# A hybrid backbone on one core: tiles moved by a few bytes in SBUF, a new start-up order, and idle products of the identity

## The chip, the cores and the metric

The kernel runs on one core of one Trainium2 chip. The metric is device time in microseconds. In the profile PE is TensorE (matrix products), PEld its loads of the stationary operand, DVE is VectorE, ACT is ScalarE, POOL is GpSimd and SP is the queue that issues the DMAs.

## The reference, cut to what matters

Two streams of 256 tokens of width 1024 (context and latent) pass four layers. The mixers are: gated delta net (layer 0), short convolution (1), differential attention (2), gated delta net (3). A squared-ReLU MLP follows each. Everything is float32.

```python
for i in range(DEPTH):                                   # DEPTH = 4, D = 1024
    mod = silu(c) @ ada_w[i] + ada_b[i]                  # shifts, scales, gates
    h = rmsnorm(x, norm1_g[i]) * (1 + sc1) + sh1
    x = x + g1 * mixer[i % 3](h)                         # delta net, conv, attention, delta net
    h = rmsnorm(x, norm2_g[i]) * (1 + sc2) + sh2
    x = x + g2 * (square(relu(h @ w1)) @ w2)             # w1: 1024 x 4096
return rmsnorm(x, final_g)                               # latent tokens; in layer 3 the context is dropped
```

## The kernel before

Activations lie transposed: eight tiles `x0..x7` of 128 features by 512 tokens (context in columns 0 to 255, latent in 256 to 511). Float32 products are split: `h` is kept as `hh` + `hl`, a weight tile as `whi` + `wlo`, and `prod` issues three products in the float32r type: hh by whi, hl by whi, hh by wlo. In a row `ch<-u,wlo`, `u` is the moving operand that streams through the array, `wlo` the stationary one, and `ch`, `mm` and `po` are PSUM banks. A product has 512 columns when both streams are computed together and 256 when one is. Every product has its own load of the stationary operand (128 columns).

Weights come as 512 KB tiles `raw` through SP. `splitter` casts them on ACT (`whi`) and subtracts on DVE or POOL (`wlo`). The last weight tiles of a stage go to tiles of their own, `whix0..` and `wlox0..`, in the stage's pool.

`mlp` runs eight rounds `f`. Each computes four blocks of `h @ w1` (4 x 8 x 3 = 96 products), squares them into `u` (`u_fin`), and then multiplies the `u` of the round before with `w2` (8 blocks x 4 x 3 = 96 products). So 96 products on `hh`/`hl` and 96 on `u` alternate. In layers 0 to 2 both kinds have 512 columns, but for the last `w2` round, which takes `whix`/`wlox` and 256 columns; in layer 3 all have 256.

The delta net keeps its per-head outputs in `y` and `NT`, the convolution in `yh` and `yl`; products with the output weights read those.

At the start `consts` loads `cv` (the conditioning vector), `more_consts` the eight `x` tiles and `pack` (all small constants), and `ada` streams 16 tiles `adaw` of the modulation weights, each followed by eight narrow passes on PE (`ch<-adaw,s`). `first_squares` sums the squares of `x` in `nacc` for the first norm. The products of layer 0's first four weight tiles (`joint`) are interleaved with those of `adaw`. When the 16 tiles are used, `opened` is set and the delta net opens its pool; the other 32 modulation tiles (`Z<-in_ada_w`) go through its ring of `Z` slots.

The order on every engine is written by a list scheduler (`Issue.run`): strands with priorities yield operations, and the one with the earliest modelled start is emitted. So a changed cost or a new strand changes what follows. Semaphores keep each engine's order as emitted.

Of the kernel before, what the change touches and what calls it, by code (L numbers as in the profile page):

```python
# [397 lines left out]
class Net:  # L398
# [4 lines left out]
    HP, DHP = -20, -20  # L403
    SHARE = 0.7
    RAW = 3
    RINGS = (dict(u=4, kt=2, E=2, qd=1, NT=2, scr=2, Z=5, gate=2, o=3, NY=1),
             dict(u=4, kt=3, E=3, qd=3, NT=3, scr=3, Z=4, gate=4, o=4, NY=1))

    def __init__(self, tc, ctx, a, depth=4):
        self.tc, self.nc, self.ctx, self.a, self.depth = tc, tc.nc, ctx, a, depth  # L410
        self.I = Issue(tc.nc)
        pool = lambda name, bufs, **k: ctx.enter_context(tc.tile_pool(name=name, bufs=bufs, **k))
        self.cp = pool("cp", 1)
        self.wp = pool("wp", 1)
# [3 lines left out]
        self.whome, self.wheld, self.wpool = [], deque(), None  # L418
# [47 lines left out]
    def splitter(self):  # L466

        I = self.I
        for n, (ap, kc, cols) in enumerate(self.wlist):
            self.pump_raw()  # L470
            home = self.whome[n]
            if home:
                yield [self.wt[n], lambda: BIG if self.wpool is None else 0.0]
            else:
                yield [self.wt[n], lambda: BIG if sum(m > self.wdone for m in self.wheld) >= self.NW else 0.0,
                       lambda: I.slot(self.wp, "whi", self.NW) - 300.0]
                self.wheld.append(n)
# [12 lines left out]
            self.wsplit = n + 1  # L490
# [249 lines left out]
    def norm_strand(self, i, which, st, half, h):  # L740

        I = self.I
        yield from self.norm_rs(st, half)
        rs, r, c = st["rs"][half], 1 - half, HALF[half]
        if "A" not in st:
# [4 lines left out]
        for k in range(NCH):  # L750
# [13 lines left out]
            B = mod[:, 24 * which + k, r:r + 1]  # L764
            yield I.act(h[0][k][:, c], tmp, AF.Identity, bias=B)
            if late:
                yield I.stt(*late)
                I.rel(late[1])
            late = (h[1][k][:, c], tmp, B, h[0][k][:, c].bitcast(F32), ALU.add, ALU.subtract)
        yield I.stt(*late)  # L770
        I.rel(late[1])
        st["hev"][half].on = True

    def norm_start(self, i, which, st, halves=(0, 1)):
        I = self.I
        h = ([], [])
        for k in range(NCH):
            h[0].append(I.tile(self.sp, f"hh{k}", [P, TT], F32R))
            h[1].append(I.tile(self.sp, f"hl{k}", [P, TT], F32R))
        st["hev"] = [Event(), Event()]  # L780
        st["h"] = h
        for half in halves:
            I.spawn(self.norm_strand(i, which, st, half, h), 3 + half)


# [6 lines left out]
    def block(self, wn, rhs, kc, cols, ps, s=slice(0, P), m=P, off=0):  # L792


        c = slice(cols.start - off, cols.stop - off)
        yield [self.have(wn)]
# [4 lines left out]

    def joint(self, wns, rhs, parts=HALF):

# [7 lines left out]
        for c in parts:  # L811
            for k in range(NCH - self.LATE if c is parts[-1] else NCH):
                for wn, ps in group:
                    yield from self.joint_prod(wn, ps, rhs, c, k)
        return group, rhs, parts[-1]

    def joint_prod(self, wn, ps, rhs, c, k):
        yield [self.have(wn)]
        wh, wl = self.wt[wn]
        m = wh.shape[-1]  # L820
        yield [wh, wl, rhs[0][k][:, c], rhs[1][k][:, c]]
        yield from self.prod(ps[0:m, c], wh[:, k, :], wl[:, k, :], rhs[0][k][:, c], rhs[1][k][:, c], k == 0, k == NCH - 1)

    def joint_end(self, group, rhs, c, fin):

        for n, (wn, ps) in enumerate(group):
            for k in range(NCH - self.LATE, NCH):
                yield from self.joint_prod(wn, ps, rhs, c, k)
            self.done(wn)
# [55 lines left out]
    def mlp(self, i, t0, st, nst, pl):  # L885
# [3 lines left out]
        h = st["h"]  # L889
        first = yield from self.joint(pl[0, 0], h, [HALF[x] for x in halves])  # L890
        with self.tc.tile_pool(name=f"mlp{i}", bufs=1) as up:
            us = {}
            self.wpool = up
            ada = Event(i + 1 == self.depth)
# [6 lines left out]
            def u_fin(f, m, ps):  # L901
                yield [lambda: I.slot(up, "r", 2)]
                r = I.tile(up, "r", [P, TT], F32, 2, True)
                u = I.tile(up, "u", [P, TT], F32, 2, True)
                yield I.act(r[:, cols], ps[:, cols], AF.Relu)
                I.rel(ps)
                yield I.act(us[f][0][m][:, cols], r[:, cols], AF.Square)
                yield I.act(u[:, cols], r[:, cols], AF.Square)
                yield I.vtt(us[f][1][m][:, cols], u[:, cols], us[f][0][m][:, cols].bitcast(F32), ALU.subtract)
                I.rel(r, u)  # L910

            nf = FF // 512
            for f in range(nf):
# [3 lines left out]
                for m in range(0 if f else 4, 4):  # L917
                    yield [self.mm_slot()]
                    ps = self.mm_ps()
                    yield from self.block(pl[0, f][m], h, NCH, cols, ps)  # L920
                    self.done(pl[0, f][m])
                    I.spawn(u_fin(f, m, ps), 2)
                if f:
                    yield from self.proj_rounds(i, pl[1, f - 1], 4, 2, us.pop(f - 1), t0, 40, None)
            if i + 1 < self.depth:
                self.norm_start(i + 1, 0, nst)
            yield from self.proj_rounds(i, pl[1, nf - 1], 4, 2, us.pop(nf - 1), t0, 40, nst)
            self.wpool = None
# [19 lines left out]
    def sconv_mixer(self, i, j, st, nst, pl):  # L948
# [3 lines left out]
        with self.tc.tile_pool(name=f"sc{i}", bufs=1) as sc:  # L952
            self.wpool = sc
            yh = [I.tile(sc, f"yh{m}", [P, TT], F32R) for m in range(NCH)]
# [66 lines left out]
    def gdn_mixer(self, i, j, last, st, nst, pl):  # L1021
# [6 lines left out]
        with self.tc.tile_pool(name=f"gd{i}", bufs=1) as gp:  # L1028
# [15 lines left out]
            for step, s in enumerate(self.ORDER[j]):  # L1044
# [27 lines left out]
                else:  # L1072
# [3 lines left out]
                    if final:  # L1076
                        self.norm_start(i, 1, nst, (1,) if t0 else (0, 1))
                    y = [sum((list(self.y[m // 2][x]) for m in heads[::2]), []) for x in range(2)]
# [277 lines left out]
    def gated(self, n, o):  # L1356
# [8 lines left out]
        if last:  # L1365

            yield [self.made[H - 1], self.free("NT", 2)] if 3 not in self.y else []
            if 3 not in self.y:
                y = [self.take("NT", [P, 2, TT], F32R) for x in range(2)]
                self.y[3] = [[y[x][:, m, :TT - t0] for m in range(2)] for x in range(2)]  # L1370
# [228 lines left out]
    def diff_head(self, n, qk, evs):  # L1599
# [38 lines left out]
        I.rel(po)  # L1638
        if n // 4 not in self.y:
            self.y[n // 4] = tuple([I.tile(dp, f"y{x}{m}", [P, TT], F32R, self.NYD) for m in range(4)] for x in range(2))  # L1640
        yh, yl = self.y[n // 4]
# [38 lines left out]
    def trunk(self):  # L1680
# [26 lines left out]
        for k in range(NCH):  # L1707
# [4 lines left out]
            I.rel(o)  # L1712

    def first_squares(self, st, half):
        for k in range(NCH):
# [3 lines left out]
    def run(self):  # L1719
        with self.tc.manual_schedule():  # L1720
# [116 lines left out]
```

## Time and profile before

| | us |
|---|---|
| median of three timed runs (lowest, highest) | 2559.81 (2558.70, 2560.28) |
| the profiled execution's own time | 2558.65 |
| its span, first to last instruction | 2556.8 |
| PE busy in the span | 2486.0 |
| DVE, ACT, POOL busy | 1874.3, 1224.3, 381.6 |

Matmul records overlap, since products are pipelined and their ends are modelled. So the time from the start of one product to the start of the next says more than the duration of a record: a run of products that follow each other without a wait has the length of the run divided by their number as its spacing.

### The profile page before, as it was taken

How to read it: one execution, taken by the hardware profiler on the slowest of the kernel's cores; microseconds unless marked ns; L12 is line 12 of the kernel's file. 1: busy time of each engine (PE TensorE's matmuls, PEld its weight loads, DVE VectorE, ACT ScalarE, POOL GpSimd, SP SyncE). 2: the span in 40 equal slices, each digit the busy share in tenths (PEclk: the TensorE clock that was granted, in tenths of full speed). 3: DMA queues.
4: the chain of work that ended last, by engine and by line, in shares of the span. 5: the costliest groups of instructions: out<-in, count | busy, mean ns of one | idle time of the engine just before them, and what ended most of it. 6: DMA issues, size and time to landing. Idle time of an engine off the chain costs nothing.

```text
span 2556.8 us, 41944 instructions
## 1 busy us (share of the span) xinstructions
PE 2486.0 (97%) x16396; PEld 2091.7 (82%) x16396; DVE 1874.3 (73%) x3552; ACT 1224.3 (48%) x2280; POOL 381.6 (15%) x273
## 2 busy tenths in 40 slices
PE   7999999899999999999999999999999999998998
PEld 3778787888888988888889767888888978888998
DVE  5776777699955545999746666799965688786666
ACT  4675664543333333533243554543233576665554
POOL 0444534100000000000000000000000164454000
PEclk9999999899999999999999999999999999998999
DMA  7322222366634233566432322366633121122564
GB/s 295 104 67 71 93 70 84 124 222 221 209 97 124 67 93 105 198 213 216 148 93 79 95 66 70 116 203 217 209 121 125 57 68 35 51 60 83 174 184 129
DMA packets 91638, 323.30 MB, mean 126 GB/s; under 512 B 10288, under 2 KB 13872, under 8 KB 91056
## 3 DMA queue, kind: packets, MB, share of 16 engines
q1 hardware_dynamic: 91440, 320.62, 38.7%
q8 instruction: 129, 2.11, 0.3%
q14 instruction: 69, 0.57, 0.1%
HBM read 317.44 MB, written 1.05 MB: 125 GB/s over the span
## 4 chain that ended last, share of the span: by engine, by line
PE 88%; DVE 6%; ACT 3%; DMA 2%; issue 1%; POOL 0%; SPq 0%; DVEq 0%; ACTq 0%; POOLq 0%
PE ch L236 43%; PE mm L236 41%; PE po L236 2%; PE ch L244 1%; DVE Z L269 1%; DMA adaw<-in_ada_w 1%; DVE wlo L274 1%; DVE dsm L290 1%; ACT L181 1%; ACT whi L257 0%; DVE e L277 0%; DVE x L277 0%; DVE nacc L274 0%; ACT kt L253 0%; DVE e L286 0%
## 5 line engine op out<-in xcount | busy, mean ns | idle before, releaser
L257 ACT CAST whi<-raw 128x1024 fp32r<-128x1024 f32 x380 | 399.6, 1052 | 806.4 <-PE ch L236 427.7
L274 DVE TENSOR_TENSOR wlo<-raw,whi 128x1024 fp32r<-128x1024 f32 x305 | 376.1, 1234 | 228.8 <-ACT whi L257 217.7
L236 PE MATMUL mm<-hh,whi 128*128 128x512 f32 (+1 forms) x1344 | 486.0, 362 | 0.0
L236 PE MATMUL mm<-hl,whi 128*128 128x512 f32 (+1 forms) x1344 | 485.4, 361 | 0.0
L236 PE MATMUL mm<-hh,wlo 128*128 128x512 f32 (+1 forms) x1344 | 484.0, 360 | 0.9 <-DVE wlo L274 0.9
L281 DVE CUSTOM_DVE_ANT_0 adaj<-adat,adas,pack 128x1024 bf16<-128x1024 f32 x288 | 368.7, 1280 | 9.5 <-ACT adas L253 5.7
L236 PE MATMUL ch<-u,whi 128*128 128x512 f32 (+1 forms) x1024 | 287.2, 367 | 0.0
L236 PE MATMUL ch<-hh,whi 128*128 128x512 f32 (+3 forms) x784 | 281.3, 359 | 2.1 <-ACT hh L253 2.1
L236 PEld LDWEIGHTS mm<-hh,wlo 128*128 128x128 f32 x1344 | 256.5, 191 | 32.6 <-issue 4.9
L236 PEld LDWEIGHTS mm<-hh,whi 128*128 128x128 f32 x1344 | 256.7, 191 | 30.5 <-issue 3.1
L236 PE MATMUL ch<-hh,wlo 128*128 128x512 f32 (+3 forms) x784 | 281.2, 359 | 0.0
L236 PEld LDWEIGHTS mm<-hl,whi 128*128 128x128 f32 x1344 | 256.7, 191 | 29.8 <-issue 3.0
L236 PE MATMUL ch<-hl,whi 128*128 128x512 f32 (+3 forms) x784 | 280.8, 358 | 0.2 <-DVE hl L277 0.2
L300 POOL TENSOR_TENSOR wlo<-raw,whi 128x1024 fp32r<-128x1024 f32 x75 | 182.3, 2432 | 259.2 <-ACT whi L257 201.8
L236 PE MATMUL mm<-u,whi 128*128 128x512 f32 (+1 forms) x768 | 215.5, 367 | 0.0
L236 PEld LDWEIGHTS ch<-u,whi 128*128 128x128 f32 x1024 | 183.5, 188 | 34.8
L236 PE MATMUL ch<-u,wlo 128*128 128x512 f32 (+1 forms) x512 | 187.7, 367 | 0.0
L277 DVE SCALAR_TENSOR_TENSOR x<-mm,mod,x 128x256 f32<-128x256 f32 x284 | 129.3, 479 | 69.6 <-PE mm L236 69.1
L300 POOL TENSOR_TENSOR qk<-qk,rope 128x512 f32<-128x512 f32 x8 | 14.0, 1754 | 1099.0 <-DMA rt<-qk 1063.0
L236 PEld LDWEIGHTS <-Z 128*128 128x128 f16 x3072 | 136.3, 98 | 46.7 <-issue 33.5
L236 PEld LDWEIGHTS ch<-hh,whi 128*128 128x128 f32 (+1 forms) x784 | 147.0, 187 | 25.5 <-ACT hh L253 3.6
L236 PEld LDWEIGHTS ch<-hh,wlo 128*128 128x128 f32 (+1 forms) x784 | 146.8, 187 | 23.2 <-issue 1.7
(259 smaller groups left out, 4544.9 us busy)
## 6 DMA issues: line engine op xcount, KB each, us to landing
raw<-in_mlp_w SPq DMA_DIRECT2D x256, 512.0 KB, 3.6
adat<-in_ada_wT SPq DMA_DIRECT2D x144, 512.0 KB, 4.6
raw<-in_gdn_w_in SPq DMA_DIRECT2D x64, 512.0 KB, 3.6
Z<-in_ada_w SPq DMA_DIRECT2D x32, 512.0 KB, 5.0
raw<-in_sconv_w_in SPq DMA_DIRECT2D x24, 512.0 KB, 3.5
raw<-in_diff_w_in SPq DMA_DIRECT2D x24, 512.0 KB, 4.0
adaw<-in_ada_w SPq DMA_DIRECT2D x16, 512.0 KB, 9.5
raw<-in_gdn_w_out SPq DMA_DIRECT2D x16, 512.0 KB, 3.6
```

The costliest lines, as they stand in the source:

```text
L181: self.nc.scalar.preload_act_table_set(self.loaded)
L236: op = Op("PE", c, [out], [lhsT, rhs], lambda: self.nc.tensor.matmul(out, lhsT=lhsT, rhs=rhs, start=start, stop=stop, **k), LAT["PE"])
L244: op = Op("PE", 107, [out], [in_, ident], lambda: self.nc.tensor.transpose(out, in_, ident), LAT["PE"])
L257: lambda: self.nc.scalar.copy(out=out, in_=in_), LAT["ACT"])
L269: op = self.vec(self._n(data), 130, [out], [data], lambda: self.nc.vector.copy_predicated(out=out, mask=mask, data=data))
L274: return self.vec(self._n(in0), 68, [out], [in0, in1], lambda: self.nc.vector.tensor_tensor(out=out, in0=in0, in1=in1, op=op))
L277: return self.vec(self._n(in0), 130, [out], [in0, in1, scalar], lambda: self.nc.vector.scalar_tensor_tensor(out=out, in0=in0, scalar=scala ...
L281: return self.vec(self._n(in0), 130, [out, junk], [in0, in1, init], lambda: self.nc.vector.tensor_tensor_reduce(out=junk, in0=in0, in1=in1 ...
L290: return self.vec(self._n(in_), 68, [out], [in_], lambda: self.nc.vector.tensor_reduce(out=out, in_=in_, axis=AX.X, op=op))
L300: lambda: self.nc.gpsimd.tensor_tensor(out=out, in0=in0, in1=in1, op=op))
```

## The change

- `consts` loads the Exp table right after the first Silu (`I.table(AF.Exp)`), and `x` becomes four tiles `x2` of 128 x 2 x 512, loaded by four DMAs of 512 KB in place of eight of 256 KB.
- The cast of `sel` from `pack` on DVE moves from `more_consts` to `load_masks`, behind the opening of the delta net's pool.
- `warm`, a strand of the lowest priority, issues products of the bf16 identity with itself (256 columns, into `po`) whenever PE has nothing else by the scheduler's model, until `opened` is set: 117 of them.
- Unused tiles `pad` of 32 n bytes per partition are put ahead of some tiles, and `SHIFT` moves the layer 3 columns of `h`, `y[3]` and `u` inside their tiles. `u_fin` squares `r` in place and needs three `r` slots in place of two `r` and two `u`.

The built kernels show what the paddings do. Take the start address (bytes in a partition) of the moving operand minus that of the stationary one, modulo 256, and call it the distance. The 10800 float32r products of both kernels, without the last rows' few of the 32-column weight tile:

| products | columns | count | distance before | after |
|---|---|---|---|---|
| hh, hl | 512 | 4092 | 0 | 0 |
| u (layers 0 to 2) | 512 | 2016 | 128 | 0 |
| y | 512 | 192 | 32 or 224 | 0 |
| yh, yl | 512 | 96 | 128 | 0 |
| hh, hl of layers 0 to 2 | 256 | 1488 | 0 | 0 |
| hh, hl of layer 3 | 256 | 768 | 0 | 192 |
| u by whix, wlox; yh, yl | 256 | 864 | 0 | 192 |
| u of layer 3 | 256 | 672 | 128 | 192 |
| y, NT | 256 | 576 | 32, 128 or 224 | 192 or 0 |

From the first MLP on the order of instructions on PE, DVE and ACT is that of before; in layer 0's mixer it differs in many places. ACT has 46 table loads, before 56.

```diff
@@ consts
-        self.x = [self.const(f"x{k}", [P, TT]) for k in range(NCH)]
+        I.table(AF.Exp)
+        self.x2 = [self.const(f"x{k}", [P, 2, TT]) for k in range(NCH // 2)]
+        self.x = [x[:, o, :] for x in self.x2 for o in range(2)]
@@ more_consts
-        for k in range(NCH):
-            I.load(self.x[k], a["xT"][:, k, :])
+        for k in range(NCH // 2):
+            I.load(self.x2[k], a["xT"][:, 2 * k:2 * k + 2, :])
         I.load(self.pack, a["pack"])
-        I.do(I.vcopy(self.sel, self.sel32))
@@ load_masks
         yield [self.free("Z", 2)]
+        yield I.vcopy(self.sel, self.sel32)
@@ paddings
+    SHIFT = 48
+    def pad(self, pool, n):
+        self.I.tile(pool, "pad", [P, 8 * n])
...
+            if home == self.hpad:
+                self.pad(pool, 2)
...
+        if i == 0 and which == 0:
+            self.pad(self.sp, 4)
...
+            if not self.y:
+                self.pad(self.gp, 9 if t0 else 11)
@@ mlp
-                yield [lambda: I.slot(up, "r", 2)]
-                r = I.tile(up, "r", [P, TT], F32, 2, True)
-                u = I.tile(up, "u", [P, TT], F32, 2, True)
+                yield [lambda: I.slot(up, "r", 3)]
+                r = I.tile(up, "r", [P, TT], F32, 3, True)
                 yield I.act(r[:, cols], ps[:, cols], AF.Relu)
                 I.rel(ps)
-                yield I.act(us[f][0][m][:, cols], r[:, cols], AF.Square)
-                yield I.act(u[:, cols], r[:, cols], AF.Square)
+                yield I.act(us[f][0][m][:, ucols], r[:, cols], AF.Square)
+                yield I.act(r[:, cols], r[:, cols], AF.Square)
@@ idle products
+    def warm(self):
+        I = self.I
+        ps = I.tile(self.psp, "po", [P, TT], F32, 1, True)
+        b = self.identb[:, None, :].to_broadcast([P, 2, P])
+        while not self.opened.on:
+            yield I.mm(ps[:, 0:T].rearrange("p (b c) -> p b c", b=2), self.identb, b, True, True)
+        I.rel(ps)
...
+            self.I.spawn(self.warm(), 9000)
```

PE's first instructions before, at the program's start (`adaw` is a modulation tile, `nacc` the sum of squares, `x4` four products in one row):

```order
L236 MATMUL ch_203<-adaw_123,s_3_74 32x256 x4
L236 MATMUL ch_203<-adaw_125,s_3_74 32x256 x4
L236 MATMUL ch_238<-adaw_127,s_3_74 32x256 x4
L244 MATMUL ch_246<-ident_86,adar_233 128x128 x2
L236 MATMUL ch_245<-nacc_66_183,ones_93 128x256
L236 MATMUL ch_238<-adaw_129,s_3_74 32x256 x4
```

The same place after the change, the end of the first 53 idle products (`po<-identb`) and what follows:

```order
L236 LDWEIGHTS identb_88
L236 MATMUL po_106<-identb_88 128x256
L236 MATMUL ch_277<-adaw_116,s_3_74 32x256 x4
L236 MATMUL ch_276<-nacc_64_177,ones_90 128x256
L236 MATMUL ch_283<-nacc_65_178,ones_90 128x256
L236 MATMUL ch_277<-adaw_118,s_3_74 32x256 x4
L236 LDWEIGHTS identb_88
L236 MATMUL po_106<-identb_88 128x256
```

The sums over `nacc` moved from behind the third modulation tile to behind the first. Behind the next tiles stand 4, 3, 8 and 35 idle products, then 6, 6 and 1 around the fifth to the seventh tile.

DVE's first instructions before (`selb` is the cast from `pack`):

```order
L266 CAST identb_91<-ident_86 128x128
L286 TENSOR_SCALAR mask_21_102<-tri_20_100 128x128
L286 TENSOR_SCALAR mask_23_106<-tri_22_104 128x128
L266 CAST selb_99<-pack_85 96x16
L274 TENSOR_TENSOR nacc_66_183<-nacc_66_183,ntmp_68_187 128x256
L274 TENSOR_TENSOR nacc_67_184<-nacc_67_184,ntmp_69_188 128x256
```

And after:

```order
L266 CAST identb_88<-ident_83 128x128
L286 TENSOR_SCALAR mask_17_99<-tri_16_97 128x128
L286 TENSOR_SCALAR mask_19_103<-tri_18_101 128x128
L274 TENSOR_TENSOR nacc_64_177<-nacc_64_177,ntmp_66_180 128x256
L274 TENSOR_TENSOR nacc_65_178<-nacc_65_178,ntmp_67_185 128x256
L274 TENSOR_TENSOR nacc_64_177<-nacc_64_177,ntmp_68_198 128x256
```

The cast is no longer ahead of the sums; it stands some 70 rows later.

PE near the end of layer 0's mixer before, where the last modulation tiles are used (`y` and `NT` are the mixer's outputs):

```order
L236 MATMUL mm_6000<-NT_5919,whi_5519 128x256
L236 MATMUL mm_6000<-NT_5920,whi_5519 128x256
L236 MATMUL mm_6000<-NT_5919,wlo_5520 128x256
L236 MATMUL ch_6010<-Z_5958,s_3_74 32x256 x4
L236 MATMUL mm_6000<-NT_5919,whi_5519 128x256
L236 MATMUL mm_6000<-NT_5920,whi_5519 128x256
```

And after, at the first such tile in that part:

```order
L236 MATMUL mm_5992<-hh_57_170,wlo_5374 128x512
L236 MATMUL ch_6037<-Z_5988,s_3_74 32x256 x4
L236 MATMUL ch_6037<-Z_5990,s_3_74 32x256 x4
L244 MATMUL ch_6058<-ident_83,adar_6054 128x128 x2
L236 MATMUL mm_6082<-y_1067_5638,whi_5623 128x256
L236 MATMUL mm_6082<-y_1069_5640,whi_5623 128x256
```

Before, four tiles stand together and a fifth nine products behind them, in the first output block. After, two stand ahead of the first output block and the next comes 144 output products later. Ten other tiles of this kind stand together earlier in the mixer, among the state updates of the first heads.

## Rows read from the trace of the kernel before

**Rows 1.** The page: span, PE's busy time, shares of the chain by engine.

```profile
span 2556.8 us, 41944 instructions
PE 2486.0 (97%) x16396; PEld 2091.7 (82%) x16396; DVE 1874.3 (73%) x3552; ACT 1224.3 (48%) x2280; POOL 381.6 (15%) x273
...
PE 88%; DVE 6%; ACT 3%; DMA 2%; issue 1%; POOL 0%; SPq 0%; DVEq 0%; ACTq 0%; POOLq 0%
```

**Rows 2.** Groups by form, PE: operands, shape, count | busy us, mean ns | idle.

```profile
L236 PE MATMUL ch<-u,whi 128*128 128x512 f32 x768 | 241.2, 395 | 0.0
...
L236 PE MATMUL mm<-u,whi 128*128 128x512 f32 x576 | 180.9, 395 | 0.0
L236 PE MATMUL ch<-u,wlo 128*128 128x512 f32 x384 | 151.7, 395 | 0.0
...
L236 PE MATMUL mm<-u,wlo 128*128 128x512 f32 x288 | 113.8, 395 | 0.0
```

**Rows 3.** Windows, products on `u`: us, PE busy (count), clock, DMA share, GB/s.

```profile
533.35:555.74 22.39, 22.39 (x96) 1.00 0.60 195
820.74:834.16 13.42, 13.42 (x113) 1.00 0.14 40
2385.58:2396.97 11.39, 11.39 (x96) 1.00 0.68 219
```

**Rows 4.** Windows, all of PE, stretches without a wait and longer ones.

```profile
555.74:577.51 21.77, 21.77 (x97) 1.00 0.69 235
...
2396.97:2408.47 11.50, 11.50 (x98) 1.00 0.62 186
1622.88:1636.14 13.26, 13.26 (x114) 1.00 0.15 41
75.00:350.00 275.00, 273.59 (x2475) 1.00 0.24 77
...
500.00:2050.00 1550.00, 1540.90 (x7721) 1.00 0.43 140
```

**Rows 5.** Timeline of PE at the start: start, us, count [idle before, releaser].

```profile
12.86 2.24 PE L236 MATMUL ch<-adaw,s 128*32 128x256 f32 x16 [12.86 <-DMA adaw<-in_ada_w]
...
22.04 0.64 PE L236 MATMUL ch<-adaw,s 128*32 128x256 f32 x8 [3.06 <-DMA adaw<-in_ada_w]
...
24.48 1.08 PE L236 MATMUL ch<-adaw,s 128*32 128x256 f32 x8 [0.67 <-DMA adaw<-in_ada_w]
...
39.25 0.64 PE L236 MATMUL ch<-adaw,s 128*32 128x256 f32 x8
```

**Rows 6.** Windows, all of PE, over two stretches of lower granted clock.

```profile
23.83:30.65 6.82, 6.17 (x33) 0.50 1.03 420
453.90:460.73 6.83, 4.83 (x26) 0.50 0.36 139
```

**Rows 7.** Chain of waits at the start: start, us, what, count.

```profile
24.48 1.08 PE ch L236 x8
...
31.00 0.57 PE ch L236 x8
```

**Rows 8.** Chain of waits near the end of layer 0's mixer.

```profile
451.17 4.59 DMA Z<-in_ada_w
...
455.90 1.08 PE ch L236 x8
```

**Rows 9.** Timeline of the start, DVE, ACT and SP.

```profile
1.25 3.74 SPq L323 DMA_DIRECT2D x<-in_xT  x8
...
2.98 0.22 DVE L266 CAST identb<-ident 128x128 bf16<-128x128 f32 x1
...
11.52 0.17 DVE L266 CAST selb<-pack 96x16 bf16<-96x16 f32 x1 [8.05 <-DMA pack<-in_pack]
11.60 4.77 DVE L274 TENSOR_TENSOR nacc<-nacc,ntmp 128x256 f32<-128x256 f32 x14
...
18.50 1.28 ACT L181 ACT_TABLE_LOAD   x1
```

More of the change, by code (lines that the diff above doesn't have):

```diff
@@ L743, in norm_strand @@
         yield from self.norm_rs(st, half)
-        rs, r, c = st["rs"][half], 1 - half, HALF[half]
+        rs, r, c, ch = st["rs"][half], 1 - half, HALF[half], self.cut(HALF[half], st["off"])
         if "A" not in st:
@@ L768, in norm_strand @@
                 I.rel(late[1])
-            late = (h[1][k][:, c], tmp, B, h[0][k][:, c].bitcast(F32), ALU.add, ALU.subtract)
+            late = (h[1][k][:, ch], tmp, B, h[0][k][:, ch].bitcast(F32), ALU.add, ALU.subtract)
         yield I.stt(*late)
@@ L772, in norm_strand, with norm_start @@
         st["hev"][half].on = True
-    def norm_start(self, i, which, st, halves=(0, 1)):
+    def norm_start(self, i, which, st, halves=(0, 1), off=0):
         I = self.I
+        st["off"] = off
         h = ([], [])
@@ L783, in norm_start, with cut @@
             I.spawn(self.norm_strand(i, which, st, half, h), 3 + half)
+    @staticmethod
+    def cut(c, off):
+        return slice(c.start - off, c.stop - off)
     def prod(self, ps, ah, al, bh, bl, first, last):
@@ L792, in block @@
     def block(self, wn, rhs, kc, cols, ps, s=slice(0, P), m=P, off=0):
-        c = slice(cols.start - off, cols.stop - off)
+        c = self.cut(cols, off)
         yield [self.have(wn)]
@@ L813, in joint, with joint_prod @@
                 for wn, ps in group:
-                    yield from self.joint_prod(wn, ps, rhs, c, k)
-        return group, rhs, parts[-1]
-    def joint_prod(self, wn, ps, rhs, c, k):
+                    yield from self.joint_prod(wn, ps, rhs, c, k, off)
+        return group, rhs, parts[-1], off
+    def joint_prod(self, wn, ps, rhs, c, k, off):
         yield [self.have(wn)]
@@ L820, in joint_prod, with joint_end @@
         m = wh.shape[-1]
-        yield [wh, wl, rhs[0][k][:, c], rhs[1][k][:, c]]
-        yield from self.prod(ps[0:m, c], wh[:, k, :], wl[:, k, :], rhs[0][k][:, c], rhs[1][k][:, c], k == 0, k == NCH - 1)
-    def joint_end(self, group, rhs, c, fin):
+        xh, xl = (rhs[x][k][:, self.cut(c, off)] for x in range(2))
+        yield [wh, wl, xh, xl]
+        yield from self.prod(ps[0:m, c], wh[:, k, :], wl[:, k, :], xh, xl, k == 0, k == NCH - 1)
+    def joint_end(self, group, rhs, c, off, fin):
         for n, (wn, ps) in enumerate(group):
             for k in range(NCH - self.LATE, NCH):
-                yield from self.joint_prod(wn, ps, rhs, c, k)
+                yield from self.joint_prod(wn, ps, rhs, c, k, off)
             self.done(wn)
@@ L889, in mlp @@
         h = st["h"]
-        first = yield from self.joint(pl[0, 0], h, [HALF[x] for x in halves])
+        off = st["off"]
+        ucols = self.cut(cols, off)
+        first = yield from self.joint(pl[0, 0], h, [HALF[x] for x in halves], off)
         with self.tc.tile_pool(name=f"mlp{i}", bufs=1) as up:
             us = {}
-            self.wpool = up
+            self.wpool, self.hpad = up, "" if t0 else "x0"
             ada = Event(i + 1 == self.depth)
@@ L919, in mlp @@
                     ps = self.mm_ps()
-                    yield from self.block(pl[0, f][m], h, NCH, cols, ps)
+                    yield from self.block(pl[0, f][m], h, NCH, cols, ps, off=off)
                     self.done(pl[0, f][m])
@@ L923, in mlp @@
                 if f:
-                    yield from self.proj_rounds(i, pl[1, f - 1], 4, 2, us.pop(f - 1), t0, 40, None)
+                    yield from self.proj_rounds(i, pl[1, f - 1], 4, 2, us.pop(f - 1), t0, 40, None, off)
             if i + 1 < self.depth:
                 self.norm_start(i + 1, 0, nst)
-            yield from self.proj_rounds(i, pl[1, nf - 1], 4, 2, us.pop(nf - 1), t0, 40, nst)
+            yield from self.proj_rounds(i, pl[1, nf - 1], 4, 2, us.pop(nf - 1), t0, 40, nst, off)
             self.wpool = None
@@ L1076, in gdn_mixer @@
                     if final:
-                        self.norm_start(i, 1, nst, (1,) if t0 else (0, 1))
+                        self.norm_start(i, 1, nst, (1,) if t0 else (0, 1), T - self.SHIFT if t0 else 0)
                     y = [sum((list(self.y[m // 2][x]) for m in heads[::2]), []) for x in range(2)]
@@ L1369, in gated @@
                 y = [self.take("NT", [P, 2, TT], F32R) for x in range(2)]
-                self.y[3] = [[y[x][:, m, :TT - t0] for m in range(2)] for x in range(2)]
+                s = self.SHIFT if t0 else 0
+                self.y[3] = [[y[x][:, m, s:s + TT - t0] for m in range(2)] for x in range(2)]
         elif n // 2 not in self.y:
+            if not self.y:
+                self.pad(self.gp, 9 if t0 else 11)
             self.y[n // 2] = tuple([I.tile(self.gp, f"y{x}{m}", [P, TT - t0], F32R, self.NY) for m in range(2)] for x in range(2))
@@ L1639, in diff_head @@
         if n // 4 not in self.y:
+            if not self.y:
+                self.pad(dp, 5)
             self.y[n // 4] = tuple([I.tile(dp, f"y{x}{m}", [P, TT], F32R, self.NYD) for m in range(4)] for x in range(2))
```

12 lines of the change are left out of this document (6 added, 6 removed).

## The prediction

> **What bounds the kernel now.** I read the page first: of a span of 2556.8 us PE is busy for 2486.0, and the chain that ends last lies on PE for 88% [rows 1]. Records of pipelined products overlap, so I looked next at windows. From 500 to 2050 us PE has work in 1540.9 of 1550 us, and inside layer 0's mixer in 273.59 of 275 [rows 4]. DVE, ACT and the DMAs hardly show there. So a change pays if PE's products come at a shorter spacing, or if one of PE's few waits goes. I then asked for two things: the spacing by kind of product, and where the clock or a wait takes PE's time.
>
> Spacing. The MLP of layers 0 to 2 alternates between 96 products on `hh`/`hl` and 96 on `u`, both of 512 columns, both at a granted clock of 1.00. A window that starts and ends with a run of `u` holds 96 of them in 22.39 us [rows 3], which is 233.2 ns each; the run of `h` behind it takes 21.77 us [rows 4], 226.8 ns each. Nothing waits in either. The record's own duration (395 ns for `u`, [rows 2]) would not have shown this. In the table of the change, what differs is the distance: 128 for `u`, 0 for `h`. For 256 columns it is the other way round: 112 products of `u` by `whix` at distance 0 take 13.42 us, 119.8 ns (the window counts one that began just before), and 96 of `u` by `whi` at 128 take 11.39 us, 118.6 ns [rows 3]. 96 on `h` at 0 take 11.50, 119.8 ns, and 112 on `y` at 224 take 13.26, 118.4 ns [rows 4]. So the same `u` buffers, at another distance to their weights, give another spacing.
>
> Waits. At the start PE idles until 12.86 us, for the first modulation tile, and again until 22.04 and 24.48 [rows 5]. Behind these gaps it is granted the lower level, 0.50 of the 2.4 GHz, that is 1.2 GHz, from 23.83 to 30.65 us, with 6.17 us of work in it [rows 6]. Eight passes take 1.08 us there and 0.57 us at 31.00 [rows 7]. From 24.48 PE has no more gap, so it runs behind the DMAs: the sixteenth tile is used at 39.25 [rows 5]. Near the end of layer 0's mixer PE waits 4.59 us for a `Z` tile [rows 8], and again has 0.50 of the clock from 453.90 to 460.73, with 4.83 us of work [rows 6].
>
> **The change, part by part.** The sum is made against the profiled execution's own 2558.65 us; the median of the runs shown is 1.16 us above it.
>
> *512 columns.* 2016 products on `u` (768 + 576 + 384 + 288, [rows 2]) go from distance 128 to 0. That is 21 runs of 96. If the distance sets the spacing, each run falls from 22.39 to 21.77: 21 x 0.62 = **-13.0**. Bounds: nothing, if something else slows `u`, and 13.0. I take the whole, because the 256-column rows move with the distance too. The 288 products on `y`, `yh` and `yl` would give 288 x 6.4 ns = 1.8; some stand beside waits, so **-1.2**. ACT and DVE must deliver 2.8% faster in these runs; their work is far from full there, as PE's lack of gaps says.
>
> The Trainium skill speaks against this term: its page "TensorE: Matmul & The Clock Gate", section "Step-by-step: what each phase is for", says that PE reads the streaming operand and the next weights through two independent SBUF ports, so that loading weights takes nothing from the running product. By that rule the distance is without effect, the terms for 512 and 256 columns are zero, and the sum would be 2552.5. The trace does not agree: 22.39 against 21.77 us.
>
> *256 columns.* 1632 products go from distance 0 to 192, and 672 from 128 to 192. No row has 192. The nearest, 224, has 118.4 ns; 128 has 118.6 and 0 has 119.8. From above I bound it by 119.8 (a gain of nothing, a loss of 672 x 1.2 ns = 0.8), from below by an estimate, half of a good 512-column product, 113.4 (1632 x 6.4 + 672 x 5.2 ns = 13.9). I take 118.4, the nearest row: 2.3 + 0.1. Against that, 384 products on `y` and `NT` go to 0, 384 x 1.4 ns = 0.5. Together **-1.9**.
>
> *Start.* The idle products keep PE at work ahead of the first tile and between the next ones. 53 of them stand ahead of the first tile. A 256-column product takes about 119 ns, so at full clock they take 6.3 us and at half clock 12.7 us; they can start when `identb` is cast, at 3.2 [rows 9], and end between 9.5 and 15.9. At worst they hold the first tile up by 3 us, which the gap before 22.04 takes up. The 35 before the fifth tile take 4.2 us at full clock, which ends near 22. The tiles land 1.22 us apart (22.04 to 24.48, two steps, [rows 5]), so the sixteenth cannot be used before 24.48 + 9 x 1.22 = 35.5. Until then PE has 9 groups of 0.57 and some 20 products of 0.227, 9.7 us, and a few transposes. If the clock stays at 2.4 GHz, PE keeps up and uses that tile at about 36.0 in place of 39.25. What follows is as much as before, so **-3.2**. The work in the cold stretch says the same: 6.17 us at half rate hold 3.1 us too much.
>
> The moved cast frees DVE: now it waits until 11.52 for `pack`, with the sums over `x` queued behind it, which end at 16.37 [rows 9]. They come several us earlier, but the fifth tile at 22.04 hides that; without the cover it would be part of the same 3.2. The table load (1.28 us at 18.50, [rows 9]) goes to a time when ACT waits for `x`. Four loads of `x` in place of eight save SP some 4 x 0.47 us of its 3.74 us of issue [rows 9], but the DMA share is 1.03 at 420 GB/s in the stretch behind [rows 6], so nothing for that. The in-place square makes the second square wait for the first; the `u` is read one run of 21.77 us later, so nothing.
>
> *The new order of layer 0's mixer.* The late modulation tiles no longer stand five deep at one place. The wait of 4.59 us and the half clock behind it (4.83 / 2 = 2.4) may go: -7.0. But ten tiles now stand together earlier, and each may bring a wait of the same kind. ACT loses ten table loads, 12.8 us in all, which PE's work hides. Bounds -8 and +8; I take **-3**.
>
> Sum: 2558.65 - 13.0 - 1.2 - 1.9 - 3.2 - 3 = 2536.35; as a median 2537.5.
>
> **Rivals.**
> 1. *The distance is not what slows `u`* (it may be the place in memory, or who wrote the tile). Then only the start and the order count: 2558.65 - 6.2 + 1.16 = 2553.6. For it: only `h` of the 512-column kinds is at 0, so the rows cannot part name from distance. Against it: `u` by `whix` and by `whi` differ. Chance 0.10. (It is what that rule of the Trainium skill would give.)
> 2. *Distance 192 is much better for 256 columns*, at 113.4 ns: 11.5 us less than my sum, 2526.0. For it: nothing but that no row excludes it. Against it: 224 and 128 lie within 1.4 ns of 0 [rows 3, 4]. Chance 0.15.
> 3. *The idle products do not do what they are for*: the clock still falls before 30 us, or they stand in the way. Then 3.2 us stay, and up to 3 are added: 2540.7 to 2543.7. For it: the first tiles' arrival, at which the idle products must be over, is only 3 us above their latest end. Chance 0.10.
> 4. *Slower*: PE waits at the ten early tiles as it did at 451 us, 4.59 + 2.4 = 7.0 us for each pair. Without the -3 the sum is 2539.35, or 2540.5 as a median; it takes four such waits to pass the old time by 5.1, and five give 2575.5. For it: three pairs stand within some 27 rows of PE, among products of the state chain that cannot cover a DMA. Against it: the scheduler put them where it sees PE wait anyway. Chance 0.04.
>
> **Numbers.** My forecast has 0.61 of the chance. About 0.2%, 5.1 us, is what a measurement of this kernel can tell from no change. Forecast, rivals 2 and 3 and half of rival 1 are faster: 0.61 + 0.15 + 0.10 + 0.05 = 0.91; I give 0.03 of that to an unlucky order on top of a smaller gain, so 0.88 faster, 0.07 same, 0.05 slower. The range goes from 2523, just under rival 2, to 2551, which takes in rival 3 and an order that costs 8 us.
>
> **What the new profile would show.** Runs of 96 products on `u` of 21.8 us, as `h`; if they stay at 22.4, term one is wrong. Layer 3's runs of 256 columns at 11.37 us or less; above 11.5 the choice of 192 costs. A granted clock of 1.00 from about 8 to 40 us and the sixteenth `adaw` group near 36 us. No wait of some 4.6 us for `Z` near the mixer's end. The run of `h` that starts at 555.74 [rows 4] would start near 549 (6.2 from the start and the order, 0.6 from the run of `u` ahead of it).

## The result, and the profile after

The changed kernel takes 2532.32 us (median of four runs, 2530.94 to 2533.99), the kernel before 2560.05 in the same comparison: a ratio of 0.9893, 95% interval 0.9875 to 0.9910. The forecast was 2537.5. The profiled execution took 2530.94 us. Its page, against [rows 1]:

```profile
span 2528.9 us, 42163 instructions
PE 2473.7 (98%) x16513; PEld 2086.5 (83%) x16513; DVE 1866.6 (74%) x3545; ACT 1225.0 (48%) x2277; POOL 381.7 (15%) x273
```

The span is 27.9 us shorter. Windows over products on `u` alone (us, PE, PEld, DVE, ACT and POOL busy, clock, DMA share, GB/s), the same three runs as in [rows 3]:

```profile
530.20:551.96 21.76, 21.76 (x96) 17.84 (x95) 0.69 (x1) 0.63 (x1) 0.00 (x0) 1.00 0.66 226
813.08:826.27 13.19, 13.19 (x113) 13.14 (x111) 0.00 (x0) 0.00 (x0) 0.00 (x0) 1.00 0.14 41
2365.80:2376.68 10.88, 10.88 (x96) 10.85 (x96) 0.84 (x2) 0.84 (x2) 0.00 (x0) 1.00 0.72 230
```

And over all of PE, the runs of [rows 4]:

```profile
551.96:573.72 21.76, 21.76 (x97) 18.02 (x96) 20.95 (x32) 9.50 (x14) 0.00 (x0) 1.00 0.62 215
...
2376.68:2387.56 10.88, 10.88 (x98) 10.88 (x97) 6.54 (x9) 7.56 (x13) 0.00 (x0) 1.00 0.65 198
1609.91:1623.34 13.43, 13.43 (x114) 13.43 (x113) 9.06 (x19) 4.36 (x9) 0.00 (x0) 1.00 0.14 41
```

Since the order from the first MLP on is that of before, the starts of the same runs show where the time went. The first run of `u` starts 3.15 us earlier (533.35 to 530.20), the first one by `whix` 7.66 earlier (820.74 to 813.08), the run on `y` 12.97 (1622.88 to 1609.91), the first run of `u` in layer 3 19.78 (2385.58 to 2365.80), the end 27.9. So 3.15 come from the start and layer 0's mixer, and 21 x 0.63 = 13.2 from the 512-column runs on `u`. The other 11.5 are 256-column products: in layer 3 six runs of `h` (11.50 to 10.88) and seven of `u` (11.39 to 10.88) give 3.7 + 3.6, the joint products ahead of them and the last round by `whix` about 1.9; each last round of layers 0 to 2 gives 0.74, three of them 2.2.

The start, PE's timeline (start, us, what, count, idle before), to be read beside [rows 5]:

```profile
3.44 8.34 PE L236 MATMUL po<-identb 128*128 128x256 bf16 x53 [3.44 <-DVE identb L266]
11.71 0.64 PE L236 MATMUL ch<-adaw,s 128*32 128x256 f32 x8
...
17.39 3.98 PE L236 MATMUL po<-identb 128*128 128x256 bf16 x35
21.79 0.64 PE L236 MATMUL ch<-adaw,s 128*32 128x256 f32 x8 [0.41 <-DMA adaw<-in_ada_w]
...
36.98 0.64 PE L236 MATMUL ch<-adaw,s 128*32 128x256 f32 x8
```

When the first 53 idle products end, the first tile is there; it is used at 11.71, before at 12.86. The clock in the stretch that had 0.50 before, and at the mixer's end:

```profile
23.83:30.65 6.82, 6.82 (x61) 2.91 (x59) 4.21 (x14) 2.85 (x7) 0.00 (x0) 1.00 1.02 407
```

```profile
479.40:486.22 6.82, 4.17 (x27) 2.39 (x27) 6.01 (x19) 4.49 (x12) 0.00 (x0) 0.50 0.63 226
```

The wait of [rows 8] is gone from its place. Two of the four modulation tiles of the mixer's end are now used after its last output product, in PE's timeline (`nacc` is the sum of squares for the next norm):

```profile
478.75 0.67 PE L236 MATMUL ch<-nacc,ones 128*128 128x256 f32 x2 [2.97 <-DVE nacc L274]
481.39 1.08 PE L236 MATMUL ch<-Z,s 128*32 128x256 f32 x8 [1.97 <-DMA Z<-in_ada_w]
482.66 1.08 PE L236 MATMUL ch<-Z,s 128*32 128x256 f32 x8 [0.19 <-DMA Z<-in_ada_w]
```

In the kernel before, the same place has the wait for `nacc` too, and the lower clock behind it; only the waits for `Z` are new there:

```profile
485.23 1.22 PE L236 MATMUL ch<-nacc,ones 128*128 128x256 f32 x2 [3.34 <-DVE nacc L274]
```

```profile
484.81:491.64 6.83, 6.41 (x28) 6.24 (x29) 6.37 (x20) 4.53 (x10) 0.00 (x0) 0.51 0.85 308
```

### The profile page after: what moved, and what is told of

Read it like the earlier page. It is cut to its first block, busy times and chain, and to the rows that moved or that the text cites. A ratio compares the mean times of both kernels' runs of the same rounds, so it can differ in the third digit from the quotient of the medians.

```text
span 2528.9 us, 42163 instructions
## 1 busy us (share of the span) xinstructions
PE 2473.7 (98%) x16513; PEld 2086.5 (83%) x16513; DVE 1866.6 (74%) x3545; ACT 1225.0 (48%) x2277; POOL 381.7 (15%) x273
## 4 chain that ended last, share of the span: by engine, by line
PE 70%; DVE 7%; ACT 3%; issue 1%; DMA 1%; POOL 0%; SPq 0%; ACTq 0%; DVEq 0%; POOLq 0%
PE ch L236 36%; PE mm L236 32%; PE po L236 1%; DVE x L277 1%; DVE nacc L274 1%; PE ch L244 1%; ACT ntmp L253 1%; DVE dsm L290 1%; DVE wlo L274 1%; DVE Z L269 1%; DVE e L277 0%; ACT whi L257 0%; DVE ntmp L277 0%; DVE e L286 0%; ACT nacc L253 0%
## 5 line engine op out<-in xcount | busy, mean ns | idle before, releaser
L236 PE MATMUL ch<-u,whi 128*128 128x512 f32 (+1 forms) x1024 | 280.4, 361 | 0.0
L236 PE MATMUL mm<-u,whi 128*128 128x512 f32 (+1 forms) x768 | 210.4, 361 | 0.0
```

Source lines behind the costliest of these rows:

```text
L236: op = Op("PE", c, [out], [lhsT, rhs], lambda: self.nc.tensor.matmul(out, lhsT=lhsT, rhs=rhs, start=start, stop=stop, **k), LAT["PE"])
```

## The experiments

The first theory is the prediction's: the distance between the two operands sets the spacing. Its rival is its first rival, another cause for the slow `u`. Two kernels halve the change, one maps the distance, one takes the idle products out.

**One distance for each round of the MLP.** `UOFF` has an offset in elements for each layer and round.

```diff
-                us[f] = tuple([I.tile(up, f"u{x}{m}", [P, TT], F32R, 2) for m in range(4)] for x in range(2))
+                o = self.UOFF[i][f]
+                us[f] = tuple([I.tile(up, f"u{x}{m}", [P, TT + 64], F32R, 2)[:, o:o + TT] for m in range(4)] for x in range(2))
```

> As the changed kernel, but the tiles u are 64 elements wider and each round of the MLP puts its u at another place inside them, so that the runs of 96 products on u stand at 21 distances for 512 columns (0 to 240, layers 0 to 2) and 7 for 256 columns (layer 3), with everything else where it was (the ring of the modulation rows in the MLP has three slots in place of four). Theory, the spacing of a run is set by the distance alone: for 512 columns 21.76 us at 0 and 22.39 at 128, for 256 columns 10.88 at 192, 11.39 at 128 would be expected, 11.50 at 0; at the distances that no row has so far, values between these. Rival, the place of the buffers or the in-place square is what helped: all runs on u of 512 columns stay at 21.8 us and those of 256 at 10.9, whatever their distance.

It took 2551.42 us (one run). Windows over its products on `u`, 96 in each, at distances 0, 128, 64, 12, 4 (512 columns), then 192, 224, 32, 64, 0 (256 columns, layer 3):

```profile
532.58:554.34 21.76, 21.76 (x96) 17.83 (x95) 0.69 (x1) 0.64 (x1) 0.00 (x0) 1.00 0.66 223
708.31:730.70 22.39, 22.39 (x96) 17.83 (x95) 0.69 (x1) 0.63 (x1) 0.00 (x0) 1.00 0.32 94
620.30:642.29 21.99, 21.99 (x96) 17.84 (x95) 0.69 (x1) 0.63 (x1) 0.00 (x0) 1.00 0.59 198
1867.30:1889.28 21.98, 21.98 (x96) 17.81 (x95) 0.69 (x1) 0.64 (x1) 0.00 (x0) 1.00 0.38 116
1778.62:1801.34 22.72, 22.72 (x96) 17.82 (x95) 0.69 (x1) 0.64 (x1) 0.00 (x0) 1.00 0.57 192
```

```profile
2382.91:2393.79 10.88, 10.88 (x96) 10.85 (x96) 0.84 (x2) 0.42 (x1) 0.00 (x0) 1.00 0.79 229
2404.68:2416.03 11.35, 11.35 (x96) 11.30 (x96) 0.47 (x2) 0.42 (x1) 0.00 (x0) 1.00 0.64 187
2449.34:2460.54 11.20, 11.20 (x96) 11.16 (x96) 0.47 (x2) 0.42 (x1) 0.00 (x0) 1.00 0.63 190
2471.44:2482.75 11.31, 11.31 (x96) 11.26 (x96) 0.47 (x2) 0.42 (x1) 0.00 (x0) 1.00 0.61 188
2426.94:2438.44 11.50, 11.50 (x96) 11.46 (x96) 0.47 (x2) 0.42 (x1) 0.00 (x0) 1.00 0.61 185
```

The same buffers, names and squares give 21.76 to 22.72 us by where in the buffer the columns stand: the rival falls. For 512 columns 0 is the best of the 21 distances, 12 and 64 come next, 128 is among the slow ones, as 192 is (22.39). For 256 columns it is 192 in this execution, and 0 is among the slowest. Each distance was timed in one run of one execution. The expectation that all values would lie between those of 0 and 128 was wrong: 4 is worse than 128. The map moves `u` alone, so for 512 columns it does not tell the distance from the start address of `u` by itself. For 256 columns the kernel before does: `u` by `whix` starts at 0 modulo 256 and `h` at 128, both are at distance 0, and both take 119.8 ns. By the rule of the Trainium skill that the prediction weighed (its page "TensorE: Matmul & The Clock Gate", section "Step-by-step: what each phase is for": loading the next weights takes no read bandwidth from the running product) all these runs would be equally long; the trace does not agree.

**The two halves.** The paddings alone, with the start of before, and the start alone, without paddings (an empty `pad`, SHIFT 0, the old squares):

```diff
-            self.I.spawn(self.warm(), 9000)     # paddings alone; x loads, table and cast also as before
...
-    SHIFT = 48                                  # start alone
+    SHIFT = 0
```

> The kernel before with the paddings, SHIFT and the in-place square alone: the old start, no idle products; PE's products stand in the order of before. In the changed kernel's trace the start of the run of h behind the first run of u was 3.8 us earlier than before and the end 27.9, so the part behind it is 24.1 and with that run's own 0.6 some 24.7 belong to the paddings if the two halves of the change add up: 2560.0 - 24.7 = 2535.3. Rival, the halves do not add (the paddings need the new order or the clock): above 2540.

> The changed kernel without paddings, SHIFT 0, with the old squares: only the moved cast, early table, four x loads and idle products; PE's products stand in the order of the changed kernel. If the halves add: 2560.0 - 3.1 = 2556.9, the sixteenth modulation tile near 37.0 us, u runs back at 22.39. As predicted it would have been 6.2 below, 2553.9. Rival, the start's gain is lost again by the two late modulation tiles in any layout: 2558 to 2560.

Measured: paddings alone 2537.88 us, ratio 0.9914 (0.9901 to 0.9927), 22.1 below before; start alone 2556.98, ratio 0.9987 (0.9978 to 0.9995), 3.0 below. Together 25.1, of 27.7 measured for the whole. The halves add up within what such comparisons tell. The traces part them cleanly: with the paddings alone the first run of `u` takes 21.76 us and layer 3's first 10.88, as in the changed kernel; with the start alone the run of `u` takes 22.39, as before. In the kernel with the paddings alone the clock is at 0.50 from 22.24 to 32.47 us and the sixteenth tile is used at 40.6; in the one with the start alone at 36.8.

**Without the idle products.**

```diff
-            self.I.spawn(self.warm(), 9000)
```

> The changed kernel without the idle products. Without them the scheduler writes the order of before behind the first hundred products, so the modulation tiles of layer 0's mixer stand late again. Theory, the idle products hold the clock up and buy the 2 to 3 us of the start, and the order gives next to nothing: sixteenth modulation tile back near 39 us, clock 0.50 somewhere in 20 to 31 us, time 2532.3 + 2.5 = 2534.8. Rival, the four loads, the cast and the table give the start: sixteenth tile near 37, 2532 to 2533. Other rival, the new order costs more than the idle products give: below 2531.

It took 2538.27 us, ratio 0.9909 (0.9895 to 0.9922), with six executions from 2530.92 to 2542.40. Two windows of the profiled one, layer 3's first run of `u`, and the start:

```profile
2369.63:2380.94 11.31, 11.31 (x99) 11.31 (x98) 8.95 (x14) 5.70 (x8) 0.00 (x0) 1.00 0.71 213
21.60:28.42 6.82, 6.05 (x35) 1.94 (x31) 4.07 (x9) 2.23 (x5) 0.00 (x0) 0.50 1.02 408
```

The clock falls again and the sixteenth tile comes at 38.6, 1.6 us later than in the changed kernel. In all eleven kernels of this document that have the idle products the clock stays at 1.00 there and this tile is used between 36.8 and 37.6; in the three without them (this one, the kernel before and the paddings alone) the clock falls to 0.50 and the tile is used at 38.6, 39.25 and 40.6: the idle products do hold the clock. But the first row was not expected. The built kernel has the same 10800 float32r products as the changed one, at the same addresses in the same order, and the run takes 11.31 us, not 10.88. All fourteen runs of 96 in layer 3's MLP stand at 117.8 ns here, and at 113.3 in the changed kernel's profile. So 256 columns at distance 192 have two spacings. They part the two profiled executions by 6 us in layer 3 alone, so the totals do not price the idle products.

**Earlier tiles, and the stationary operand moved.** The next four test the two open points: what the late modulation tiles cost, and whether the other 256-column products can be brought to 192. `SHARE` sets how many modulation tiles have a high priority by each part of the mixer. For the second, weight slots get 64 elements more, and a tile that only 256-column products use stands 16 elements higher in its slot.

```diff
-    SHARE = 0.7
+    SHARE = 0.85
```

```diff
+    s = 16 if n in self.wfar else 0      # wfar: the tiles that only 256-column products use
+    t = I.tile(pool, x, [P, kc * cols + 64], F32R, bufs)[:, s:s + kc * cols]
```

> The changed kernel with SHARE 0.85 in place of 0.7, so that the last four modulation tiles of layer 0 no longer stand at the mixer's end but among its products. In the changed kernel PE stands for most of 475.5 to 484.6 us there: 3.0 us for the sum of squares, then 2.2 us for the two last Z tiles, with the clock at 0.50 behind. Theory, the two late tiles ate the gain of the new order: the first product of the MLP's joint part comes some 5 us earlier and the time falls from 2532.3 to about 2527.5. Rival, the wait is only moved to the new place of these tiles: 2531 to 2533.

> The changed kernel with the high parts of those weight tiles that only 256-column products use (the joint tiles of layers 0 to 2, the last output tiles, v and gates of layer 3) put 64 bytes higher in their slots; hh and hl stay where they are. So the distance of 1200-odd products goes from 0 to 192 by the stationary operand's address alone, that of their low parts stays 0. To make room for the slots some paddings move: 96 products on y of 512 columns go to 32, and y and NT of layer 3 to 64, which costs about 1.5 us. The order is that of the changed kernel. Theory, the distance between the two operands counts: the joint runs of the convolution, 121.0 ns a product, fall to about 116.7, the total to 2532.3 - 7.9 + 1.5 = 2526. Rival, the address of the moving operand alone counts: 121.0 ns, 2533 to 2534.

> The same with the low parts put 64 bytes higher and the high parts left: one product of three goes to distance 192. Theory, each product's spacing goes by its own distance: joint runs at about 118.8 ns a product, 2532.3 - 3.9 + 1.5 = 2530. Rival, what counts is the weights that are loaded while a product streams, those of the next one: the mean is the same, but the short gap stands behind hl in place of behind the product on wlo.

> Both parts 64 bytes higher, SHARE 0.85, and one slot in place of two for adar (to make room), so the order in layer 0's mixer differs from the two others. If the terms add: joint runs at 114.6 ns a product, 2532.3 - 11.8 + 1.5 - 5 = 2517. Rival, the single adar slot makes the modulation tiles wait in the mixer: 2520 to 2526.

SHARE 0.85: 2534.27 us, ratio 0.9902 (0.9887 to 0.9917): no gain. The two tiles left the end, but PE waits elsewhere, in the waits between 440 and 490 us:

```profile
PE mm L236 <- ACT NT L257: 6.8, 1, 6.8
PE ch L236 <- DVE nacc L274: 4.3, 1, 4.3
```

With the tiles gone PE waits there for the head's output and the sum of squares; the theory that the tiles alone cost 5 us falls.

The joint runs of the convolution (the products of its first four weight tiles), 96 on `hh` and `hl` in each window: the changed kernel (both parts at 0), high parts at 192, low parts at 192, both:

```profile
841.77:853.29 11.52, 11.52 (x98) 11.52 (x97) 5.99 (x14) 3.42 (x7) 0.00 (x0) 1.00 0.01 1
```

```profile
839.61:851.35 11.74, 11.74 (x99) 11.74 (x97) 5.92 (x14) 3.35 (x7) 0.00 (x0) 1.00 0.00 1
```

```profile
838.87:850.18 11.31, 11.31 (x98) 11.31 (x97) 5.89 (x14) 3.34 (x7) 0.00 (x0) 1.00 0.01 1
```

```profile
847.75:858.63 10.88, 10.88 (x98) 10.88 (x97) 6.11 (x14) 3.55 (x7) 0.00 (x0) 1.00 0.01 2
```

`hh` and `hl` did not move, so the address of the moving operand alone is not what counts. But the gain is not a sum over products either: two thirds of them at 192 make the run slower, one third makes it faster, all give 113.3 ns (and 117.8 in the first kernel of the next part, which has them all as well). With the low parts alone at 192 every product stands at 117.8, those at 0 too. With the high parts alone the steps from one product to the next repeat in threes, of 118, 122 and 127 ns. The totals are 2534.75 us, ratio 0.9908 (0.9890 to 0.9926), for the high parts, 2532.59 (one run) for the low, and 2533.98, ratio 0.9903 (0.9888 to 0.9918), for both; the last had 117.8 ns in layer 3, and in the mixer the same waits as with SHARE 0.85 alone (6.8 and 4.4 us), so what its single `adar` slot cost is not shown.

**Both parts in the changed kernel's order, and small products in layer 3.** `kick` issues one unused product into `po`.

```diff
+                if t0 and f:
+                    yield from kick(self.identb, self.identb, P)    # ahead of h
...
+                if t0 and f:
+                    yield from kick(self.ones, self.ident, P)       # ahead of u
```

> The changed kernel with high and low parts of the tiles that only 256-column products use 64 bytes higher, in the order of the changed kernel and with SHARE 0.7; the raw tile of the 32-column weights goes to a pool of the stage to make room. So 1848 products of 256 columns go from distance 0 to 192. In the kernels run so far a run at 192 takes one of two spacings, 113.3 or 117.8 ns a product, and keeps it until PE is interrupted; at 0 it takes 119.8. Theory, both spacings are open to any run at 192, by how the interruption before it ended: the joint runs fall from 121.0 to 114.5 or 118.9, the first half of the last MLP round keeps 117.8, the MLP of layer 3 has 113.3 in some executions and 117.8 in others, 6.0 us apart. Time 2532.3 - 4 to - 12 + 1.5: between 2521 and 2530, with executions some 6 us apart. Rival, the two spacings are a fixed property of a place in the program: executions agree within 2 us.

> The changed kernel with two small unused products in each round from the second on of layer 3's MLP: a bf16 product of the identity with itself (128 columns) ahead of each run on hh and hl, and an fp32 product of ones with the identity (128 columns) ahead of each run on u. Theory, an interruption of PE's float32r stream lets it fall into the other spacing: some of the 13 runs of 96 products change between 113.3 and 117.8 ns behind a small product, and if one kind of small product always ends in 113.3, it can be used to get there. Rival, the spacing is set once at the layer's start by the clock's return and small products leave it as it is: all runs at one spacing.

Both parts at 192: 2527.15 us, ratio 0.9879 (0.9861 to 0.9896), four executions of 2523.76, 2526.48, 2527.83 and 2534.58. It is the fastest median here, but its interval overlaps that of the changed kernel, and the two were not timed together. Its joint run of the convolution, the one shown above for the others, takes 11.31 us with all products at 192, where the kernel with both parts and SHARE 0.85 took 10.88:

```profile
839.58:850.89 11.31, 11.31 (x99) 11.31 (x97) 6.01 (x14) 3.45 (x7) 0.00 (x0) 1.00 0.00 1
```

The spread of 10.8 us fits the two spacings, but only one of the four executions has a trace, so this is not shown. The kernel with the small products took 2537.78, ratio 0.9918 (0.9902 to 0.9935). Three windows of it, 80 products each, behind a bf16, an fp32 and again a bf16 product:

```profile
2380.01:2389.43 9.42, 9.42 (x83) 9.42 (x81) 5.16 (x6) 6.15 (x12) 0.00 (x0) 1.00 0.62 192
2391.40:2400.47 9.07, 9.07 (x82) 9.07 (x81) 7.22 (x11) 4.38 (x7) 0.00 (x0) 1.00 0.60 184
2402.44:2411.86 9.42, 9.42 (x82) 9.42 (x81) 5.03 (x6) 6.17 (x12) 0.00 (x0) 1.00 0.63 190
```

117.7, 113.3 and 117.7 ns a product: each of the seven bf16 products changed the run from 113.3 to 117.7, each of the seven fp32 ones back. So the spacing is no property of the addresses alone. A small product can change it, and within a run without one it stayed.

**One small product to choose the spacing.** A bf16 one in the changed kernel, an fp32 one in the kernel with both parts at 192, ahead of the last joint products of layer 3's MLP.

```diff
                 if f == 0:
+                    if t0:
+                        yield from kick(self.identb, self.identb, P)    # or (self.ones, self.ident, P)
                     yield from self.joint_end(...)
```

> The changed kernel with one unused bf16 product of the identity (128 columns) ahead of the last part of the joint products of layer 3's MLP, everything else in the order of the changed kernel. In kick_map each of the six such products that PE was held by was followed by 117.7 ns a product, each fp32 one by 113.3. Theory: all of layer 3's runs stand at 117.8 ns; 1380 products x 4.5 ns = 6.2 us more than the profile of the changed kernel, so executions lie near 2537 to 2539 where those of the changed kernel reach from 2531 to 2534. That is also what the prediction's 256-column term would have given (118.4 taken). Rival: the product only resets the phase and the clock's return or another event picks the spacing: 2531 to 2535.

> joint_all with one unused fp32 product (ones with the identity, 128 columns) at the same place in layer 3's MLP and one ahead of the last MLP round in each of layers 0 to 2. Theory: layer 3's runs stand at 113.3 ns in every execution and the 112 products by whix in each layer fall from 117.8 to 113.3, 3 x (0.5 - 0.2) us; from the profile of joint_all (2526.5, which had 113.3 in layer 3) about 2525.5, and the executions agree within some 4 us in place of 11. Rival: the spread of joint_all came from elsewhere (the start, the clock): as wide as before, median 2527.

The bf16 one: 2537.37 us, ratio 0.9922 (0.9908 to 0.9935), five executions from 2536.19 to 2540.95. The fp32 one: 2533.66, ratio 0.9897 (0.9883 to 0.9910), 2526.53 to 2535.86. The first run of `u` in layer 3, bf16, then fp32:

```profile
2365.68:2376.99 11.31, 11.31 (x99) 11.31 (x98) 8.74 (x14) 5.50 (x8) 0.00 (x0) 1.00 0.71 219
```

```profile
2364.26:2375.57 11.31, 11.31 (x98) 11.31 (x97) 9.33 (x14) 6.26 (x10) 0.00 (x0) 1.00 0.75 220
```

The first did what was expected, and puts a price on the spacing: 5.1 us by the medians, 7.4 by the ratios (0.9922 and 0.9893 of 2560), since the two kernels were not timed together. The second missed. In its trace PE stood at 113.3 ns just ahead of the fp32 product and at 117.8 behind it, and behind the three fp32 products ahead of the last rounds the 112 products by `whix` stood at 117.8, as they do without them. So the kind of the small product does not set the spacing. In the profiled executions a small product mostly changed it, from whichever it was; but an fp32 sum-of-squares product in the convolution's output run left 117.8 as it was in five of them, the changed kernel's among these. What decides stays open.

## Why the prediction was right, and where its sum was off

The total came 5.2 us below the forecast, and that it came so near is in part luck, because two misses partly cancel: the profile gives 9.6 us more than the sum had for 256 columns, and some 4 less for the start, the order and the `y`, `yh` and `yl` products.

*512 columns, right.* 21 runs x 0.63 = 13.2 us for a forecast of 13.0, and the map shows that where `u` starts, and not the buffer or who wrote it, is the cause. The `y`, `yh` and `yl` term (1.2) is too small to be told apart.

*256 columns, mis-sized.* The forecast took 118.4 ns for distance 192, the nearest row, and came to -1.9; the profile gives about -11.5. Its lower bound of 113.4 was right to 0.1 ns, and the second rival, at 0.15, is what layer 3 did in the profiled execution. The step that failed is the use of a row at 224 for one at 192: the map has 118.2 ns (11.35 / 96) at 224 and 113.3 at 192, so neighbours say little. But a value near the one that was taken is also found, 117.8 ns: in the first 112 products of the last rounds of layers 0 to 2 in this same trace (13.19 / 112; behind the sum-of-squares product that follows, the other 80 of each round fall to 113.3), and in layer 3 of five other kernels. With layer 3 held at 117.8, the changed kernel takes 2537.37; that this is close to the forecast's 2537.5 is in part luck, since the start and the order gave less than forecast. What the forecast lacked is that one distance can have two spacings. Where layer 3 has the other one, some 5 to 7 us more are gained.

*Start, nearly right.* The clock is at 1.00 from 8.36 to 69.80 us as forecast, and the sixteenth tile is used at 36.98, not at 36.0: 2.3 us earlier, forecast 3.2. From the fifth tile to the sixteenth PE needs 15.2 us without a wait for a tile, where the estimate had 14.0 (22.04 to 36.0): what stands between the tiles takes longer than was reckoned. That the idle products end in time was right (11.71 against 12.86 before). They start 213 ns apart until 8.3 us and 109 ns apart from there, where the estimate had 119 ns at full clock, the spacing of float32r products. Rival 3's sentence has its two times the wrong way round: it is the latest end, 15.9, that lies 3 us behind the arrival at 12.86. Without the idle products the sixteenth tile comes at 38.6, so of the 2.3 us they would give 1.6, and the loads, the cast and the table the rest. But the paddings alone, with the start of before, use it at 40.6 and not at 39.25, so this split is not known to better than 1.4 us.

*Order of layer 0's mixer, off.* -3 forecast; start and order together give 3.15 at the first MLP, where 6.2 were forecast. In the trace 2.3 of these are there at the sixteenth tile, which leaves some 0.8 for the order. The wait of 4.6 us is gone, as forecast, and the half clock behind it too. Against that, PE waits 2.2 us for the two `Z` tiles at the mixer's end; the 3.0 us for the sum of squares there and the half clock behind were there before (3.34 us). Moving the two tiles away from there gave nothing. The kernel before and the one with the paddings alone have PE's products in the same order up to there, and start the first run of 96 on `h` 2.3 us apart (511.56 and 513.83), so the share of the order is not known to better than that. Against the paddings alone the changed kernel starts its first run of `u` 5.4 us earlier (535.62 to 530.20), and by the medians start and order give 3.0 (start alone) to 5.6 us (the whole against the paddings alone). That they fell short of 6.2 is likely; by how much is open.

*Rivals 3 and 4* did not come: the clock held, and no tile cost 7 us.

## What to carry to other kernels

Where PE never waits, divide a run of equal products by their number and compare runs that should be alike: a difference of 2 to 5% between two operands of the same shape can be an address, and some bytes of padding can remove it. Measure the distance for each width by itself, since the best one for 512 columns (0) is among the worst for 256, and measure it more than once: at 192 the second spacing (11.31 us for 96) is no better than the one run at 64. When executions of such a kernel differ by more than those of its predecessor, compare the spacing within long runs before looking for a wait.

## What the runs showed of the hardware that was not expected

- Products of 256 columns in float32r at distance 192 take either 113.3 or 117.8 ns at the same addresses, and kept to it for over a thousand products; long runs wholly at distance 0 took 119.8 to 120.0 in every trace, and 512 columns at 0 took 226.7 or 226.8, but for the map, where runs of `h` between runs of `u` at other distances took up to 227.2.
- One unused product of 128 columns in between can change the products behind it by 4% (113.3 to 117.8 ns), up to the next such product. What decides is open.
- A mixture of distances in one run is not a mean: two products of three at 192 and one at 0 gave 122.3 ns (11.74 / 96), above the 120.0 of all at 0.
